# First loads cut smaller and reordered; the output projection's last four weight units kept in two kinds of tiles

## The chip, the cores and the metric

One core of a Trainium2 chip runs the whole kernel. TensorE (PE) multiplies, VectorE (DVE) and ScalarE (ACT) do the elementwise work, GpSimd (POOL) and SyncE (SP) do little more than issue DMAs. The metric is the device time of one execution in microseconds (us). Three runs of the kernel before gave 444.34, 444.35 and 445.06 us; their median is 444.35 us.

## The reference

A two-layer decoder trunk over 256 tokens of width 1024, in float32. Only its two ends matter here:

```python
h = rms_norm(x, norm_g)                  # layer 0 begins
nq, nkc, ..., nz, ... = split(h @ w_in)  # "nz": 512 columns, the gate of the first head group
...
# layer 1 ends: retention output (4 heads x 512) and memory attention (256), gated
y = concat([r_out * silu(rz), m_out * silu(ez)]) @ w_out     # (256, 2304) @ (2304, 1024)
x = x + y
return rms_norm(x, final_norm_g)
```

## The kernel before

Every projection is computed with operands split into a high and a low part: a float32 weight piece arrives in a `raw` tile (six buffers, `NRAW`), ScalarE copies it into a high tile (`S.copy(hi, raw)`, line 122), VectorE subtracts to get the low tile (line 123), and TensorE adds three products, high by high, high by low, low by high (`mm3`, lines 135 to 137). The high and low tiles normally come from the tags `whi` and `wlo`, four buffers each; `split` can be told to take both from another tag, `v4`, which has nine buffers and also serves the residual rows, the last norm's gain and the layer's values and gates.

A scheduler places the instructions in each engine's queue when the kernel is built, from its own estimate of their times; each engine then works through its queue in that order. A tile whose buffers are all taken makes its first writer wait until the oldest one is read for the last time. Only the first loads are placed by hand, inside `tc.manual_schedule` (lines 264 to 279), on the queues of SP and ACT. At most eight loads of these two queues are under way at once: each holds one of eight semaphores, and the ninth waits until the first has landed. The load of `gain0` went through the queue of POOL, which is outside those eight.

**The beginning.** The first projection, "nz" (lines 281 to 293), multiplies 512 columns of weight by the 256 tokens, in eight steps `kt` of 128 rows. For each step `gain_split` (line 233) turns the raw input `xraw` into `xh` (line 237 on VectorE for step 0, line 239 on ScalarE after that) and `xl` (line 240 on VectorE), which needs the gain vector `gain0` (line 245). Before that TensorE runs six warm-up multiplications of a zero tile (line 282), each of which is two instructions in the trace. The second projection, "ksw", is the first that a helper loads: its first two weight pieces are the tiles `ahead` (line 277), and its sums go to the PSUM banks `s`. The loads that follow the weights of "nz" are, in order: vectors, constants, positions, the two pieces `ahead`, and two tiles `xrow` of token rows, whose squares (line 303) give the norm.

**The end.** `out_project` (line 683) multiplies layer 1's 18 units of 128 rows by 1024 output columns. The sums stand in four PSUM banks, `acc[tok][half]`, for two blocks of 128 tokens and two halves of 512 columns; the fourth has the tag `tr`. In the last projection (`last=True`) the last four units are not multiplied when they arrive but kept (`late`, lines 691 to 695), and lines 700 to 705 then go group by group through all four: token block 0, first half; block 0, second half; block 1, first half; block 1, columns 512 to 767; block 1, columns 768 to 1023, which has a bank of its own, `s`. As soon as a group is summed, lines 827 to 861 can take it: add it to the residual (line 839, or 836 for the last group), square it (line 841), multiply by the gain (847), then per token block a root (848), a reciprocal (849), the scaling (851 on GpSimd for block 0, 853 on ScalarE for block 1, 857 and 859 on VectorE) and the stores (860, 861).

The weight tiles of all four kept units have the tag `v4`, two for each unit, eight in all. Two more `v4` tiles hold the residual `x0` and one the gain `gf` at that time.

Of the kernel before, what the change touches and what calls it, by code (L numbers as in the profile page):

```python
# [16 lines left out]
P = 128  # L17
T = 256
D = 1024
KT = 8  # L20
# [23 lines left out]
V_G0 = 0  # L44
# [8 lines left out]
def trunk(  # L53
# [19 lines left out]
    nc = tc.nc  # L73
# [13 lines left out]
    def load(t, src):  # L87
        nc.sync.dma_start(t, src)
        return t
# [28 lines left out]
    def split(raw, cols, tag=None):  # L118

        hi = tl(tag or "whi", [P, 1024], NV if tag else 4, F32R)[:, :cols]  # L120
        lo = tl(tag or "wlo", [P, 1024], NV if tag else 4, F32R)[:, :cols]
        S.copy(hi, raw)  # L122
        V.tensor_tensor(lo, raw, hi.bitcast(F32), ALU.subtract)  # L123
        return hi, lo
# [108 lines left out]
    def gain_split(raw, g, hi, lo, k0, kts):  # L233
        for kt in kts:
            r = raw[:, kt - k0]
            if g is gain0 and kt == 0:
                V.tensor_scalar(hi[:, kt], r, g[:, kt : kt + 1], None, op0=ALU.mult)
            else:
                S.activation(hi[:, kt], r, AF.Copy, scale=g[:, kt : kt + 1])
            V.scalar_tensor_tensor(lo[:, kt], r, g[:, kt : kt + 1], hi[:, kt].bitcast(F32),  # L240
                                   op0=ALU.mult, op1=ALU.subtract)


    gain0 = tl("gain0", [P, KT])
    G.dma_start(gain0, vec[:, V_G0 : V_G0 + KT])
    warm = tl("p", [P, 2, 512], 2)[:, 0]
    V.memset(warm, 0.0)
    seed = tl("seed", [P, 1])
# [13 lines left out]
            xraw.append(tl("raw", [P, 1024], NRAW).rearrange("p (k t) -> p k t", k=4))  # L262
        wraw.append(tl("raw", [P, 1024], NRAW))
    with tc.manual_schedule(engines={mybir.EngineType.SP, mybir.EngineType.Activation}):
        load(wraw[0][:, 0:512], w512[0][:, 0:512])
        nc.scalar.dma_start(xraw[0][:, 0:1], xT[:, 0:1])
        nc.scalar.dma_start(xraw[0][:, 1:2], xT[:, 1:2])
        load(wraw[0][:, 512:1024], w512[0][:, 512:1024])
        S.activation(seed, seed, AF.Sin)
        for q in range(1, 4):  # L270
            load(xraw[q // 2][:, 2 * (q % 2) : 2 * (q % 2) + 2], xT[:, 2 * q : 2 * q + 2])
            load(wraw[q], w512[q // 2][:, (q % 2) * 1024 : (q % 2 + 1) * 1024])
        load(vect, vec)
        load(cpak, cst)
        load(posi, pos)
        load(posr, posrow.to_broadcast([P, T]))
        ahead = [load(tl("raw", [P, 1024], NRAW), w512[2][:, u * 1024 : (u + 1) * 1024]) for u in range(2)]
        for tok in range(2):
            load(xrow[tok], xtok[:, tok])
    wb = bank("t")  # L280
    for _ in range(6):
        PE.matmul(wb[:, :256], warm[:, 0:P], warm[:, :256], start=True, stop=True)
    for q in range(4):
        for j in range(2):
            kt = 2 * q + j
            gain_split(xraw[q // 2], gain0, xh, xl, 4 * (q // 2), (kt,))
            wh, wl = split(wraw[q][:, j * 512 : (j + 1) * 512], 512)
            if kt > 1:
                turned_unit(ps_n, (xh, xl), wh, wl, (kt,), range(4))
                continue  # L290
            for w, x in ((wh, xh), (wh, xl), (wl, xh)):
                for ct in range(4):
                    PE.matmul(ps_n[ct // 2][:, (ct % 2) * T : (ct % 2 + 1) * T], w[:, ct * P : (ct + 1) * P], x[:, kt],
                              start=kt == 0 and ct % 2 == 0 and w is wh and x is xh, stop=False, skip_group_check=True)

    rstd0 = tl("rstd0", [P, 2])
    rq0 = tl("rq0", [P, 2])
# [381 lines left out]
    def out_project(first, ys, last=False):  # L679

        acc = [[bank("pj"), bank("pj")], [bank("pj"), bank("tr")]]
        todo = []
        for y, n in ys:
            for k0 in range(0, n, 2):
                todo.append((y, k0))
        total = len(todo)
        kept = []
        for i, (y, k0) in enumerate(todo):
            for u in range(2):
                raw = load(tl("raw", [P, 1024], NRAW), wout[first + i][:, u * 1024 : (u + 1) * 1024])  # L690
                late = last and i >= total - 2
                wh, wl = split(raw, 1024, "v4" if late else None)
                if late:
                    kept.append((y, k0 + u, wh, wl))
                    continue
                for tok in range(2):
                    for c in range(2):
                        part(acc, tok, c * 512, 512, y, k0 + u, wh, wl, i == 0 and u == 0,
                             not last and i == total - 1 and u == 1)
        if last:  # L700
            rest = bank("s")
            for tok, c0, n in ((0, 0, 512), (0, 512, 512), (1, 0, 512), (1, 512, 512 - CUT), (1, 1024 - CUT, CUT)):
                for j, k in enumerate(kept):
                    dst = [[rest, rest]] * 2 if c0 + CUT == D else acc
                    part(dst, tok, c0, n, *k, c0 + CUT == D and j == 0, j == len(kept) - 1)
            acc.append(rest)
        return acc
# [256 lines left out]
```

## Time and profile before

| | us |
|---|---|
| median of three runs | 444.35 |
| profiled execution, whole | 444.3 |
| profiled execution, span from first to last instruction | 442.5 |
| TensorE busy | 427.5 (97%) |
| VectorE busy | 312.5 (71%) |
| ScalarE busy | 250.3 (57%) |

The span is 1.8 us shorter than the time of the same execution; what lies around it is launch and end. "Busy" is the time in which an instruction ran; matmuls overlap, so a busy TensorE is not one at its peak. The chain that ended last lies to 90% on TensorE, which means that nearly all of the span is one engine's queue. In timelines, "[idle before <-releaser]" says how long the engine had been idle ahead of the row and what ended it. The tile names leave the buffer numbers out, and some lose their digits: `v` is the tag `v4`, `gain` is `gain0`.

### The profile page before, as it was taken

To read this page: it belongs to the slowest core of one execution; us is meant where nothing else is said; L and a number is where in the kernel's file an instruction comes from. 1 tells how busy PE (TensorE), PEld (TensorE's weight loads), DVE (VectorE), ACT (ScalarE), POOL (GpSimd) and SP (SyncE) were. 2 spreads that over 40 slices of the span, in tenths; PEclk is the share of its full clock that TensorE was granted. 3 is DMA by queue.
4 is the path that set the end of the run, shared out by engine and by line. 5 is a ranking of instruction groups with operands and counts; after the bars stand their busy time and mean duration, and the time that the engine had idled before them with its cause. 6 is when DMAs were issued, how large, how long until landed. Compare 5 with 4: busy or idle time off the path is not lost.

```text
span 442.5 us, 6757 instructions
## 1 busy us (share of the span) xinstructions
PE 427.5 (97%) x2450; PEld 353.8 (80%) x2450; DVE 312.5 (71%) x734; ACT 250.3 (57%) x463; POOL 4.2 (1%) x10
## 2 busy tenths in 40 slices
PE   8999999999999899999999999999999999999991
PEld 7988999788776577669987878888888888888871
DVE  4899695995578765739688874676998467586315
ACT  5775537765649866837566544556355535546123
POOL 1000000000000000000000000000000000000001
PEclk9999999999999999999999999999999999999997
DMA  8975956654435314334464454655466553656002
GB/s 270 391 265 171 381 164 204 221 184 128 157 97 198 135 47 144 96 107 130 146 209 138 148 177 142 189 175 191 129 207 200 171 168 121 230 191 190 1 0 95
DMA packets 30081, 74.22 MB, mean 168 GB/s; under 512 B 2784, under 2 KB 14048, under 8 KB 30048
## 3 DMA queue, kind: packets, MB, share of 16 engines
q1 hardware_dynamic: 29584, 73.27, 50.3%
q10 hardware_dynamic: 432, 0.52, 0.4%
q8 instruction: 19, 0.31, 0.3%
q14 instruction: 14, 0.11, 0.1%
q0 software_dynamic: 32, 0.00, 0.0%
HBM read 72.74 MB, written 1.05 MB: 167 GB/s over the span
## 4 chain that ended last, share of the span: by engine, by line
PE 90%; DVE 4%; DMA 2%; ACT 1%; issue 1%; POOLq 0%; ACTq 0%
PE pj L136 18%; PE pj L135 17%; PE pj L137 17%; PE pj L181 8%; PE pj L182 4%; PE t L216 4%; PE s L100 4%; PE o L100 3%; PE tr L136 1%; PE tr L135 1%; DVE wlo L123 1%; DMA raw<-in_memtok 1%; PE tr L137 1%; PE s L136 1%; PE s L135 1%; PE s L137 1%
## 5 line engine op out<-in xcount | busy, mean ns | idle before, releaser
L123 DVE TENSOR_TENSOR wlo<-raw,whi 128x1024 fp32r<-128x1024 f32 (+2 forms) x124 | 144.6, 1172 | 59.8 <-ACT whi L122 58.5
L122 ACT CAST whi<-raw 128x1024 fp32r<-128x1024 f32 (+2 forms) x124 | 124.7, 1009 | 91.8 <-PE pj L137 40.4
L136 PE MATMUL pj<-wlo,big 128*128 128x512 f32 (+2 forms) x264 | 99.5, 377 | 0.1
L137 PE MATMUL pj<-whi,big 128*128 128x512 f32 (+2 forms) x264 | 98.2, 373 | 0.0
L135 PE MATMUL pj<-whi,big 128*128 128x512 f32 (+2 forms) x264 | 98.2, 375 | 0.0
L137 PEld LDWEIGHTS pj<-whi,big 128*128 128x128 f32 x264 | 49.7, 188 | 8.7 <-issue 0.3
L135 PEld LDWEIGHTS pj<-whi,big 128*128 128x128 f32 x264 | 49.7, 188 | 8.7 <-DVE wlo L123 0.4
L181 PE MATMUL pj<-big,whi 128*128 128x512 f32 x160 | 56.6, 397 | 0.0
L136 PEld LDWEIGHTS pj<-wlo,big 128*128 128x128 f32 x264 | 49.7, 188 | 8.6 <-DVE wlo L123 0.3
L182 PE MATMUL pj<-big,wlo 128*128 128x256 f32 x160 | 44.7, 283 | 0.0
L181 PEld LDWEIGHTS pj<-big,whi 128*128 128x128 f32 x160 | 29.8, 188 | 6.7 <-DVE tmp L356 0.3
L135 PE MATMUL pj<-big,whi 128*128 128x256 f32 x120 | 34.4, 288 | 0.1
L136 PE MATMUL pj<-big,whi 128*128 128x256 f32 x120 | 34.4, 287 | 0.0
L137 PE MATMUL pj<-big,wlo 128*128 128x256 f32 x120 | 34.1, 284 | 0.0
L182 PEld LDWEIGHTS pj<-big,wlo 128*128 128x128 f32 x160 | 30.2, 189 | 1.1 <-issue 0.7
L135 PEld LDWEIGHTS pj<-big,whi 128*128 128x128 f32 x120 | 22.8, 191 | 0.9 <-DVE v L723 0.5
L136 PEld LDWEIGHTS pj<-big,whi 128*128 128x128 f32 x120 | 22.9, 191 | 0.8 <-issue 0.7
L137 PEld LDWEIGHTS pj<-big,wlo 128*128 128x128 f32 x120 | 22.9, 191 | 0.0
L405 ACT ACTIVATE p<-p,mx 128x128 f32<-128x128 f32 (+1 forms) x48 | 21.3, 447 | 0.9 <-DVE mx L403 0.9
L417 ACT COPY pt<-t 128x384 f32<-128x384 f32 x24 | 11.5, 479 | 18.1 <-PE t L216 18.0
L216 PE MATMUL t<-cst,p 128*128 128x128 f32 x104 | 18.1, 284 | 0.6 <-ACT pt L417 0.6
L123 DVE TENSOR_TENSOR v<-raw,v 128x1024 fp32r<-128x1024 f32 x4 | 4.9, 1225 | 19.1 <-ACT v L122 19.1
(297 smaller groups left out, 656.8 us busy)
## 6 DMA issues: line engine op xcount, KB each, us to landing
raw<-in_w SPq DMA_DIRECT2D x91, 512.0 KB, 4.2
raw<-in_wout SPq DMA_DIRECT2D x28, 512.0 KB, 3.9
v<-in_xtok SPq DMA_DIRECT2D x4, 512.0 KB, 7.2
raw<-in_w SPq DMA_DIRECT2D x4, 280.0 KB, 3.6
v<-in_w SPq DMA_DIRECT2D x2, 512.0 KB, 6.9
raw<-in_memT SPq DMA_DIRECT2D x2, 512.0 KB, 4.8
raw<-in_memtok SPq DMA_DIRECT2D x2, 512.0 KB, 4.8
v<-in_grow SPq DMA_DIRECT2D x2, 512.0 KB, 7.3
```

The source lines that it names most:

```text
L100: ins = PE.matmul(out, lhs, rhs, start=start, stop=stop)
L122: S.copy(hi, raw)
L123: V.tensor_tensor(lo, raw, hi.bitcast(F32), ALU.subtract)
L135: PE.matmul(ps, lh, rh, start=start, stop=False, skip_group_check=shared)
L136: PE.matmul(ps, lh, rl, start=False, stop=False, skip_group_check=shared)
L137: PE.matmul(ps, ll, rh, start=False, stop=stop, skip_group_check=shared)
L181: PE.matmul(ps[ct], wh[:, c], both[:, :, kt], start=kt == 0, stop=False, skip_group_check=True)
L182: PE.matmul(ps[ct][:, T:], wl[:, c], both[:, 0, kt], start=False, stop=kt == KT - 1, skip_group_check=True)
L216: PE.transpose(b[:, i * P : (i + 1) * P], a, ident)
L405: S.activation(p[:, hh, a], p[:, hh, a], AF.Exp, bias=mx[:, hh, tok : tok + 1], scale=-1.0, accum_out=sm[:, hh, tok : tok + 1])
L417: got = S.copy(pt[:, hh, :384], transposes([p[:, hh, i * P : (i + 1) * P] for i in range(3)]))
```

## The change

Five edits at the beginning and one at the end.

- `gain0` is loaded first on ACT's queue instead of on POOL's.
- The weights of step 0 (256 KB) come in two pieces of 256 columns, the first on ACT's queue, the second on SP's. The inputs of steps 0 and 1 come on SP's queue instead of ACT's, and the input of step 0 is the first load there.
- The warm-up is three multiplications instead of six.
- Step 0 is split and multiplied in two halves of 256 columns (`first_columns`); step 1 goes through the same function whole.
- `gain_split` and `split` stand in one loop over `kt`, with the same calls for steps 2 to 7.
- In the last output projection only the units of the last pair of rows (`i == total - 1`) take `v4` tiles. The first two kept units take `whi` and `wlo`.

```diff
--- before.py
+++ after.py
@@ -242,7 +242,6 @@
 
 
     gain0 = tl("gain0", [P, KT])
-    G.dma_start(gain0, vec[:, V_G0 : V_G0 + KT])
     warm = tl("p", [P, 2, 512], 2)[:, 0]
     V.memset(warm, 0.0)
     seed = tl("seed", [P, 1])
@@ -262,9 +261,11 @@
             xraw.append(tl("raw", [P, 1024], NRAW).rearrange("p (k t) -> p k t", k=4))
         wraw.append(tl("raw", [P, 1024], NRAW))
     with tc.manual_schedule(engines={mybir.EngineType.SP, mybir.EngineType.Activation}):
-        load(wraw[0][:, 0:512], w512[0][:, 0:512])
-        nc.scalar.dma_start(xraw[0][:, 0:1], xT[:, 0:1])
-        nc.scalar.dma_start(xraw[0][:, 1:2], xT[:, 1:2])
+        nc.scalar.dma_start(gain0, vec[:, V_G0 : V_G0 + KT])
+        load(xraw[0][:, 0:1], xT[:, 0:1])
+        nc.scalar.dma_start(wraw[0][:, 0:256], w512[0][:, 0:256])
+        load(wraw[0][:, 256:512], w512[0][:, 256:512])
+        load(xraw[0][:, 1:2], xT[:, 1:2])
         load(wraw[0][:, 512:1024], w512[0][:, 512:1024])
         S.activation(seed, seed, AF.Sin)
         for q in range(1, 4):
@@ -278,20 +279,26 @@
         for tok in range(2):
             load(xrow[tok], xtok[:, tok])
     wb = bank("t")
-    for _ in range(6):
+    for _ in range(3):
         PE.matmul(wb[:, :256], warm[:, 0:P], warm[:, :256], start=True, stop=True)
-    for q in range(4):
-        for j in range(2):
-            kt = 2 * q + j
-            gain_split(xraw[q // 2], gain0, xh, xl, 4 * (q // 2), (kt,))
-            wh, wl = split(wraw[q][:, j * 512 : (j + 1) * 512], 512)
-            if kt > 1:
-                turned_unit(ps_n, (xh, xl), wh, wl, (kt,), range(4))
-                continue
-            for w, x in ((wh, xh), (wh, xl), (wl, xh)):
-                for ct in range(4):
-                    PE.matmul(ps_n[ct // 2][:, (ct % 2) * T : (ct % 2 + 1) * T], w[:, ct * P : (ct + 1) * P], x[:, kt],
-                              start=kt == 0 and ct % 2 == 0 and w is wh and x is xh, stop=False, skip_group_check=True)
+    def first_columns(w, kt, c0, n):
+
+        wh, wl = split(w, n)
+        for a, x in ((wh, xh), (wh, xl), (wl, xh)):
+            for ct in range(c0 // P, (c0 + n) // P):
+                PE.matmul(ps_n[ct // 2][:, (ct % 2) * T : (ct % 2 + 1) * T], a[:, ct * P - c0 : ct * P - c0 + P], x[:, kt],
+                          start=kt == 0 and ct % 2 == 0 and a is wh and x is xh, stop=False, skip_group_check=True)
+
+    for kt in range(KT):
+        w = wraw[kt // 2][:, (kt % 2) * 512 : (kt % 2 + 1) * 512]
+        gain_split(xraw[kt // 4], gain0, xh, xl, 4 * (kt // 4), (kt,))
+        if kt == 0:
+            for c0 in (0, 256):
+                first_columns(w[:, c0 : c0 + 256], 0, c0, 256)
+        elif kt == 1:
+            first_columns(w, 1, 0, 512)
+        else:
+            turned_unit(ps_n, (xh, xl), *split(w, 512), (kt,), range(4))
 
     rstd0 = tl("rstd0", [P, 2])
     rq0 = tl("rq0", [P, 2])
@@ -689,7 +696,7 @@
             for u in range(2):
                 raw = load(tl("raw", [P, 1024], NRAW), wout[first + i][:, u * 1024 : (u + 1) * 1024])
                 late = last and i >= total - 2
-                wh, wl = split(raw, 1024, "v4" if late else None)
+                wh, wl = split(raw, 1024, "v4" if last and i == total - 1 else None)
                 if late:
                     kept.append((y, k0 + u, wh, wl))
                     continue
```

How this moves the instructions, from the order in which each engine gets them. The line numbers of the changed kernel are seven higher behind line 300.

SP's queue at the start, before; raw_77 holds the weights of steps 0 and 1, raw_76 the inputs of steps 0 to 3, raw_78 and raw_79 the next ones of each:

```order
L88 DMA raw_77<-in_w 128x512 x2
L88 DMA raw_76<-in_xT 128x512
L88 DMA raw_78<-in_w 128x1024
L88 DMA raw_79<-in_xT 128x512
L88 DMA raw_80<-in_w 128x1024
L88 DMA raw_79<-in_xT 128x512
```

and in the changed kernel, where raw_76 holds the first weights and raw_75 the first inputs:

```order
L88 DMA raw_75<-in_xT 128x256
L88 DMA raw_76<-in_w 128x256
L88 DMA raw_75<-in_xT 128x256
L88 DMA raw_76<-in_w 128x512
L88 DMA raw_75<-in_xT 128x512
L88 DMA raw_77<-in_w 128x1024
L88 DMA raw_78<-in_xT 128x512
L88 DMA raw_79<-in_w 128x1024
```

The input of step 0 comes first; the input of steps 2 and 3 (raw_75, 128x512) is the fifth issue instead of the third, and all that follows moves back by two in the same way. ACT's queue at the same place, before:

```order
L266 DMA raw_76<-in_xT 128x256
L267 DMA raw_76<-in_xT 128x256
L269 ACT_TABLE_LOAD
L269 ACTIVATE seed_65<-seed_65 128x1
L122 CAST whi_115<-raw_77 128x512
```

and now:

```order
L264 DMA gain_1_61<-in_vec 128x8
L266 DMA raw_76<-in_w 128x256
L270 ACT_TABLE_LOAD
L270 ACTIVATE seed_64<-seed_64 128x1
L122 CAST whi_113<-raw_76 128x256
L122 CAST whi_123<-raw_76 128x256
L239 ACTIVATE big_72<-raw_75,gain_1_61 128x256
L122 CAST whi_135<-raw_76 128x512
```

The gain and a quarter of the first weights take the place of two inputs, and the first cast is now two of 256 columns.

TensorE's last rows, before; v_847, v_850 and v_853 are the high tiles of the second, third and fourth kept unit, v_848, v_851 and v_854 their low tiles, pj_4024 and pj_4025 token block 0, s_4304 the last group:

```order
L135 MATMUL s_4304<-v_850_4294,y_3938 128x256
L136 MATMUL s_4304<-v_851_4295,y_3938 128x256
L137 MATMUL s_4304<-v_850_4294,y_3938 128x256
L135 MATMUL pj_4024<-v_853_4300,y_3938 128x512
L135 MATMUL pj_4025<-v_853_4300,y_3938 128x512
L135 MATMUL pj_4026<-v_853_4300,y_3938 128x512
L135 MATMUL tr_4027<-v_853_4300,y_3938 128x256
L135 MATMUL s_4304<-v_853_4300,y_3938 128x256
L136 MATMUL pj_4024<-v_854_4301,y_3938 128x512
L137 MATMUL pj_4024<-v_853_4300,y_3938 128x512
L136 MATMUL pj_4025<-v_854_4301,y_3938 128x512
L137 MATMUL pj_4025<-v_853_4300,y_3938 128x512
```

All groups go through three units; the fourth unit's fifteen matmuls stand behind the last group, its five high-by-high ones first. In the changed kernel, where pj_4026 is block 0's first half, the kept units are whi_4284, whi_4290, v_852 and v_855:

```order
L135 MATMUL pj_4026<-whi_4284,y_3940 128x512
L136 MATMUL pj_4026<-wlo_4285,y_3940 128x512
L137 MATMUL pj_4026<-whi_4284,y_3940 128x512
L135 MATMUL pj_4026<-whi_4290,y_3940 128x512
L135 MATMUL pj_4027<-whi_4284,y_3940 128x512
L136 MATMUL pj_4027<-wlo_4285,y_3940 128x512
L136 MATMUL pj_4026<-wlo_4291,y_3940 128x512
L137 MATMUL pj_4026<-whi_4290,y_3940 128x512
L135 MATMUL pj_4026<-v_852_4296,y_3940 128x512
L136 MATMUL pj_4026<-v_853_4297,y_3940 128x512
L137 MATMUL pj_4026<-v_852_4296,y_3940 128x512
L135 MATMUL pj_4026<-v_855_4302,y_3940 128x512
```

The four units now stand inside one group, and the group pj_4026 is finished before the next ones begin (two matmuls of pj_4027 stand in front). ScalarE's last casts, before:

```order
L122 CAST v_847_4288<-raw_4286 128x1024
L122 CAST whi_4228<-raw_4226 128x1024
L122 CAST v_850_4294<-raw_4292 128x1024
L795 CAST y_3938<-t_4015 128x4x128
L122 CAST whi_4246<-raw_4244 128x1024
L122 CAST whi_4264<-raw_4262 128x1024
L122 CAST v_853_4300<-raw_4298 128x1024
L825 ACT_TABLE_LOAD
L825 ACTIVATE root_4365<-root_4365 128x1
```

and now:

```order
L122 CAST v_852_4296<-raw_4294 128x1024
L802 CAST y_3940<-t_4017 128x4x128
L122 CAST whi_4248<-raw_4246 128x1024
L122 CAST v_855_4302<-raw_4300 128x1024
L832 ACT_TABLE_LOAD
L832 ACTIVATE root_4367<-root_4367 128x1
L122 CAST whi_4266<-raw_4264 128x1024
L122 CAST whi_4284<-raw_4282 128x1024
L122 CAST whi_4290<-raw_4288 128x1024
```

Before, the last cast is that of the fourth kept unit into v_853; now the two `v4` casts come early, and the last three casts fill `whi` tiles, two of them kept units. VectorE's rows behind its last split, before:

```order
L839 TENSOR_TENSOR v_388_2025<-pj_4024,v_388_2025 128x512
L839 TENSOR_TENSOR v_388_2025<-pj_4025,v_388_2025 128x512
L847 TENSOR_TENSOR p_4369<-v_388_2025,v_796_4022 128x512
L839 TENSOR_TENSOR v_389_2027<-pj_4026,v_389_2027 128x512
L839 TENSOR_TENSOR v_389_2027<-tr_4027,v_389_2027 128x512
L843 TENSOR_SCALAR ss_857_4368<-ss_857_4368 128x1
L847 TENSOR_TENSOR p_4385<-v_389_2027,v_796_4022 128x512
L847 TENSOR_TENSOR p_4385<-v_389_2027,v_796_4022 128x256
L843 TENSOR_SCALAR ss_861_4384<-ss_861_4384 128x1
L836 TENSOR_TENSOR v_389_2027<-s_4304,v_389_2027 128x256
L849 RECIPROCAL ss_857_4368<-ss_857_4368 128x1
```

and now:

```order
L846 TENSOR_TENSOR v_390_2027<-pj_4026,v_390_2027 128x512
L854 TENSOR_TENSOR p_4371<-v_390_2027,v_798_4024 128x512
L850 TENSOR_SCALAR ss_859_4370<-ss_859_4370 128x1
L846 TENSOR_TENSOR v_390_2027<-pj_4027,v_390_2027 128x512
L856 RECIPROCAL ss_859_4370<-ss_859_4370 128x1
L864 SCALAR_TENSOR_TENSOR p_4371<-v_390_2027,ss_859_4370,v_798_4024 128x512
L846 TENSOR_TENSOR v_391_2029<-pj_4028,v_391_2029 128x512
L854 TENSOR_TENSOR p_4387<-v_391_2029,v_798_4024 128x512
L846 TENSOR_TENSOR v_391_2029<-tr_4029,v_391_2029 128x512
L850 TENSOR_SCALAR ss_863_4386<-ss_863_4386 128x1
L854 TENSOR_TENSOR p_4387<-v_391_2029,v_798_4024 128x256
L843 TENSOR_TENSOR v_391_2029<-s_4306,v_391_2029 128x256
```

Before, both halves of block 0 are added one right behind the other and their reciprocal (849) comes after the last group's add (836). Now each group's add is followed by its own work, and the reciprocal of block 0 (now 856) stands ahead of block 1.

## Rows read from the trace of the kernel before

**Rows 1.** page, part 1: busy us (share of span) and instructions by engine.

```profile
PE 427.5 (97%) x2450; PEld 353.8 (80%) x2450; DVE 312.5 (71%) x734; ACT 250.3 (57%) x463; POOL 4.2 (1%) x10
```

**Rows 2.** timeline, TensorE, 0 to 25 us: start, us, engine, line, operation, tiles, count.

```profile
1.46 5.49 PE L282 MATMUL t<-p 128*128 128x256 f32 x12 [1.46 <-DVE root L824]
6.54 1.72 PE L293 MATMUL pj<-big,whi 128*128 128x256 f32 x8
8.10 0.64 PE L293 MATMUL pj<-big,wlo 128*128 128x256 f32 x4
...
18.54 0.28 PE L137 MATMUL pj<-big,wlo 128*128 128x256 f32 x1
...
19.13 0.39 PE L136 MATMUL s<-wlo,big 128*128 128x512 f32 x1
...
24.59 0.39 PE L136 MATMUL s<-wlo,big 128*128 128x512 f32 x1
```

**Rows 3.** timeline, VectorE and then ScalarE, 4 to 24 us.

```profile
6.04 0.35 DVE L237 TENSOR_SCALAR big<-raw,gain 128x256 fp32r<-128x256 f32 x1 [4.62 <-DMA gain<-in_vec]
...
17.34 1.22 DVE L123 TENSOR_TENSOR wlo<-raw,whi 128x1024 fp32r<-128x1024 f32 x1
...
23.00 1.23 DVE L123 TENSOR_TENSOR wlo<-raw,whi 128x1024 fp32r<-128x1024 f32 x1
...
8.31 1.15 ACT L122 CAST whi<-raw 128x512 fp32r<-128x512 f32 x2 [0.71 <-DMA raw<-in_w]
...
16.19 1.05 ACT L122 CAST whi<-raw 128x1024 fp32r<-128x1024 f32 x1 [2.30 <-DMA raw<-in_w]
...
20.16 1.06 ACT L303 ACTIVATE v<-v 128x1024 f32<-128x1024 f32 x1 [0.37 <-DMA v<-in_xtok]
```

**Rows 4.** busy time by stretch: PE, PEld, DVE, ACT, POOL, PEclk, DMA share, GB/s.

```profile
8.00:20.00 12.00, 12.00 (x97) 11.78 (x96) 11.02 (x24) 8.34 (x14) 0.00 (x0) 1.00 1.03 388
...
432.95:442.50 9.55, 0.00 (x0) 0.00 (x0) 4.90 (x14) 3.51 (x12) 2.04 (x1) 0.75 0.29 110
```

**Rows 5.** timeline, TensorE, 420 to 433 us.

```profile
420.66 0.39 PE L135 MATMUL pj<-v,y 128*128 128x512 f32 x1
...
426.94 0.28 PE L135 MATMUL tr<-v,y 128*128 128x256 f32 x1
...
428.96 0.28 PE L137 MATMUL s<-v,y 128*128 128x256 f32 x1
...
429.55 0.96 PE L135 MATMUL pj<-v,y 128*128 128x512 f32 x3 [0.31 <-ACT v L122]
...
432.66 0.28 PE L137 MATMUL s<-v,y 128*128 128x256 f32 x1
```

**Rows 6.** timeline, ScalarE, 408 to 430 us.

```profile
408.90 2.00 ACT L122 CAST whi<-raw 128x1024 fp32r<-128x1024 f32 x2
...
428.44 1.05 ACT L122 CAST v<-raw 128x1024 fp32r<-128x1024 f32 x1 [17.54 <-PE s L136]
```

**Rows 7.** timeline, VectorE and SyncE, 431 to 439 us.

```profile
435.63 0.41 DVE L836 TENSOR_TENSOR v<-s,v 128x256 f32<-128x256 f32 x1
...
436.93 1.43 SPq L861 DMA_DIRECT2D out_y<-p  x2
438.45 0.38 SPq L860 DMA_DIRECT2D out_y<-p  x1
```

**Rows 8.** the tile out_y, its four DMAs.

```profile
DMA to landing us min/median/max: 2.0/2.7/2.9
```

**Rows 9.** DMA issues, 0 to 20 us: line, engine, count, KB, us to landing.

```profile
raw<-in_xT ACTq DMA_DIRECT2D x1, 128.0 KB, 3.6
...
gain<-in_vec POOLq DMA_DIRECT2D x1, 4.0 KB, 4.8
```

**Rows 10.** DMA queues, 0 to 20 us: packets, MB, share of 16 engines.

```profile
q1 hardware_dynamic: 2609, 6.20, 87.5%
q10 hardware_dynamic: 288, 0.26, 4.5%
```

## The prediction, made before the changed kernel was run

> **What bounds the kernel now.** The page's first part comes first: TensorE is busy for 97% of the span [rows 1], so only the stretches count in which its queue stands, and whatever lies behind its last matmul. The timeline of its two ends shows both places of the change. At the beginning, the warm-up covers 5.49 us from 1.46, and the first real matmul starts at 6.54 [rows 2]. VectorE's timeline says what that one waits for: its first product idles 4.62 us until the gain has landed, and runs from 6.04 to 6.39 [rows 3]. From 6.54 on TensorE does not pause, but it is followed closely: the low part of the first "ksw" piece is ready at 17.34 + 1.22 = 18.56 and used at 19.13, that of the third piece is ready at 23.00 + 1.23 = 24.23 and used at 24.59 [rows 2, 3]. Those are spare times of 0.57 and 0.36 us. What paces these two is not TensorE: the first cast waited 2.30 us for its load until 16.19, the squares of the token rows waited for theirs until 20.16 [rows 3], and the 16 DMA engines are full from 8 to 20 us at 388 GB/s [rows 4].
>
> At the end, the kept units' matmuls run from 420.66; 27 of 512 columns take until 426.94 (0.2326 each), 17 of 256 until 428.96 (0.1188 each). Then TensorE waits: the three that begin at 429.55 are those of the fourth unit, and the last of its fifteen starts at 432.66 [rows 5]. ScalarE says why: it had been idle 17.54 us, until the group `s` had read an older tile, when it began the fourth unit's cast at 428.44 [rows 6]. Nothing in the tail could start earlier, since every group needs that unit. So VectorE's adds come one behind the other after TensorE's end, the last at 435.63, and SP's last store at 438.45 [rows 7]. Behind the last matmul 9.55 us of span are left without TensorE, with 4.90 us of VectorE's work in them [rows 4].
>
> **The end of the change.** Four kept units need eight `v4` tiles where six were free. Now two of them take four, and two take `whi` and `wlo`. No instruction is added. Sixty matmuls run without a pause: 36 x 0.2326 + 23 x 0.1188 = 11.11, so the last starts at 431.77, 0.89 us earlier than 432.66, and ends 0.28 later at 432.05 [rows 5].
>
> The larger part lies behind it. Block 0's groups are summed 24 and more matmuls before the end, that is by 420.66 + 24 x 0.2326 + 0.2 = 426.4; its adds, root, scaling and stores then run beside block 1's 5.6 us of matmuls. All of the tail's VectorE work is 4.90 us [rows 4], of which block 0 has about half, so it fits there. I cost it at nothing; uncovered it would cost up to 2.5. Only the last group's add is left to wait for TensorE, and can begin at 432.05 instead of 435.63: 3.58 us earlier [rows 5, 7]. What follows it is unchanged up to block 1's stores. The second one of SP's two issues starts at about 436.93 + 1.43 - 0.36 = 438.0, now 434.4. SP's store at 438.45, which waited for GpSimd's 2.04 us [rows 4, 7], belongs to block 0 and is early now. A store lands 2.0 to 2.9 us after its issue, 2.7 in the middle [rows 8]. Before, the end was 438.45 + 2.9 = 441.35, with 1.15 of span behind it; now 434.4 + 2.7 + 1.15 = 438.25. The end gives 442.5 - 438.25 = 4.25, bounded by 3.6 (only the add's shift) and 4.9 (a landing after 2.0). I take 4.2.
>
> The added waits are those of the two `whi` casts, which wait for the unit four places ahead of them. Each unit is twelve matmuls, 2.79 us, so the second one's wait ends at 420.66 - 2 x 2.79 = 415.1. A cast of 1.05 and a split of 1.22 [rows 3, 6] make 417.4, 3 us ahead of need. Between 410.9 and 428.44 ScalarE had nothing to do [rows 6]; that hides all the casts. Behind them in its queue there are only the squares of the tail. The table load moved ahead of three casts runs in the same idle stretch.
>
> **The beginning.** The warm-up's half ends at 1.46 + 5.49 / 2 = 4.2. The gain leaves POOL's queue, where it took 4.8 us from issue to landing, for ACT's, where the 128 KB issued first took 3.6 [rows 9]; issued at the start it is there by about 4.3 at the latest. So the first real matmul can start between 4.2 and 4.8, about 2 us earlier. But steps 2 and 3 need a load whose cast began at 8.31 and whose first half ends 0.6 later [rows 3]. With the same bytes ahead of it, step 2 starts at about 8.9, where now it starts at 8.10 + 16 x 0.120 = 10.02 (0.120 is 10.44 us over the 87 matmuls up to 18.54) [rows 2]. That lead of 1.1 us shrinks to 0.57 at the first "ksw" piece and to 0.36 at the third, since neither load has fewer bytes ahead of it. With a few hundredths for the hand-over I take 0.3. Behind that TensorE decides alone, and the lead is kept to the end.
>
> For the smaller pieces: the first 20 us moved 6.20 MB in q1, rows of 2 KB and more for the most part, for 87.5% of 320 us, 45 us per MB; q10's rows of 1 KB cost 4.5% of 320 us for 0.26 MB, 55 us per MB [rows 10]. The 256 KB that now come in 1 KB rows cost 0.26 x 10 / 16 = 0.17 us of the stream at most, nothing at least. I take nothing, since q1's figure contains the stalls of the start as well. The Trainium skill (DMA: Bandwidth & Descriptors, Rules for kernel authors) speaks against this half of the change: small transfers should be merged, and issuing from another engine saves only issue time, as all queues share 16 engines. By that rule alone the beginning would give nothing and the time would be 440.1; the full engines [rows 4] agree with it for everything behind step 2.
>
> The gain now holds one of the eight load semaphores, so SP waits one load sooner: the inputs of steps 4 and 5 wait for the gain, and all later loads stand behind them. The eight loads ahead hold 1.5 MB, 4 us of work at 388 GB/s [rows 4], so the engines do not run dry.
>
> **Sum.** The profiled execution has 444.3 us, 1.8 around its span; the median is 444.35. 444.3 - 4.2 - 0.3 = 439.8.
>
> **Rivals.**
> 1. *The full clock comes later.* From 6.54 to 8.10 a matmul takes 0.195, later 0.120 [rows 2], with a granted clock of 1.00 behind 8 us, the level of 2.4 GHz [rows 4]; so part of the first stretch ran at the lower level, 1.2 GHz, at 0.24 at most. The warm-up is halved, and a pause may follow it. If the full level needs the present 6.6 us (1.46 to 8.10) from 4.4 on, it comes at 11. From 4.4 on at 0.24, TensorE falls behind the old schedule after 9.9, half a us for each one: 0.5 us lost instead of 0.3 gained, 440.6. Against it: the gap is short. The Trainium skill (TensorE: Matmul & The Clock Gate, Part 1) says that the lower clock is the default and sustained activity releases it; the fall from 0.195 to 0.120 agrees, and no pause ahead of it is to be seen in this trace.
> 2. *The loads come earlier.* The first 20 us moved 6.46 MB, of which 12 x 0.388 = 4.66 fall behind 8 us [rows 4, 10], so the first 8 us moved only 1.8 MB; if the gain's small transfer on POOL's queue or the order held it back, "ksw" moves up too, and the lead of 1.1 us is kept: 439.0. Nothing but the slow start speaks for it.
> 3. *The end is held back.* ScalarE's queue has the last `v4` cast, which waits for the last load, ahead of the three `whi` casts. If that load is late, the casts are too, and TensorE pauses inside the groups; or the fourth unit still comes last and the change does not do what it says. Half of the 4.2 is lost: 442; all of it: 444. Against it stands 3 us of spare time.
> 4. *Slower.* The lower clock stays through "ksw", because the loads leave pauses in TensorE's first work. Each us behind 9.9 costs 0.5; the change is slower from 9.9 + 4.2 / 0.5 = 18.3 us on, and at 20 the time is 445.2. After 8.10 the kernel before shows no such stretch.
>
> **Chances.** Forecast 0.52 (439.4 to 440.2), first rival 0.20, second 0.15, third 0.09, slower 0.04. A third of the third rival ends within 0.2% (0.9 us, about what can be told from no change). That gives faster 0.93, same 0.03, slower 0.04. The range runs from 438.8 to 441.3: it takes in both ends of the store's landing and the first rival.
>
> **What would show it.** In the changed profile TensorE has no wait between the first kept matmul and its end, and the last matmul starts some 11.1 us after the first; behind it about 6.2 us of span are left instead of 9.55. The first real matmul starts before 5 us. The second "ksw" low-part matmul row (19.13 here) is 0.3 to 0.6 earlier, and the same lead is still there at the first kept matmul. I am wrong if that lead is gone in the middle, if TensorE pauses in the kept groups, or if block 0's stores are issued after block 1's matmuls end.

## The result, and the profile after

The changed kernel takes 440.48 us (median of five runs, 440.16 to 441.16) against 444.48 for the kernel before beside it (444.34 to 445.06): a ratio of 0.9911, 95% interval 0.990 to 0.9923. Forecast were 439.8, and 438.8 to 441.3. The profiled execution took 440.28, its span 438.5. TensorE's work is the old one less six warm-up instructions, page part 1:

```profile
PE 426.3 (97%) x2444; PEld 352.7 (80%) x2444; DVE 314.3 (72%) x735; ACT 250.7 (57%) x464; POOL 3.5 (1%) x9
```

**The end did what was forecast.** The timelines of TensorE, ScalarE, VectorE and SyncE there answer to [rows 5 to 7]:

```profile
420.99 0.40 PE L135 MATMUL pj<-whi,y 128*128 128x512 f32 x1
...
432.09 0.28 PE L137 MATMUL s<-v,y 128*128 128x256 f32 x1
...
415.57 1.05 ACT L122 CAST whi<-raw 128x1024 fp32r<-128x1024 f32 x1 [0.99 <-PE tr L137]
425.20 0.64 ACT L848 ACTIVATE rot_a<-v 128x512 f32<-128x512 f32 x1 [8.58 <-DVE v L846]
...
432.41 0.42 DVE L843 TENSOR_TENSOR v<-s,v 128x256 f32<-128x256 f32 x1 [0.25 <-PE s L137]
...
429.59 0.35 SPq L868 DMA_DIRECT2D out_y<-p  x1
...
434.77 0.33 SPq L868 DMA_DIRECT2D out_y<-p  x1
```

Sixty matmuls start within 11.10 us (420.99 to 432.09) with no wait among them. ScalarE makes its last kept cast at 415.57 and then idles 8.58 us; the cast at 428.44 of [rows 6] is gone. Block 0's first store is issued at 429.59, while TensorE works on block 1. Only the last group's add stands behind TensorE (432.41, formerly 435.63). Behind the last matmul 6.12 us are left instead of 9.55, with 1.40 us of VectorE's work instead of 4.90 [rows 4]:

```profile
432.37:438.49 6.12, 0.00 (x0) 0.00 (x0) 1.40 (x5) 1.52 (x4) 0.00 (x0) 0.74 0.26 98
```

**The beginning lost.** The first kept matmul comes at 420.99, 0.33 later than the 420.66 of [rows 5], where 0.3 earlier was forecast. TensorE's, VectorE's and ScalarE's timelines of the first 20 us, beside [rows 2, 3] (VectorE's row stands behind TensorE's):

```profile
1.45 2.93 PE L283 MATMUL t<-p 128*128 128x256 f32 x6 [1.45 <-DVE root L831]
5.04 2.07 PE L289 MATMUL pj<-big,whi 128*128 128x256 f32 x8 [0.66 <-ACT whi L122]
...
9.09 0.64 PE L289 MATMUL pj<-big,wlo 128*128 128x256 f32 x4
10.27 0.39 PE L135 MATMUL pj<-big,whi 128*128 128x256 f32 x1 [0.54 <-ACT whi L122]
...
19.72 0.40 PE L136 MATMUL s<-wlo,big 128*128 128x512 f32 x1
...
3.31 0.35 DVE L237 TENSOR_SCALAR big<-raw,gain 128x256 fp32r<-128x256 f32 x1 [1.90 <-DMA gain<-in_vec]
...
9.60 1.14 ACT L122 CAST whi<-raw 128x512 fp32r<-128x512 f32 x2 [0.43 <-DMA raw<-in_w]
...
17.20 1.05 ACT L122 CAST whi<-raw 128x1024 fp32r<-128x1024 f32 x1 [2.44 <-DMA raw<-in_w]
```

The gain is there by 3.3 us and the first real matmul, which now waits for the cast of the first weights, starts at 5.04, 1.5 earlier. But the weights of steps 2 and 3 are first cast at 9.60 instead of 8.31, step 2 starts at 10.27 instead of 10.02, and the "ksw" row, the first matmul there that reads a low weight part and a landmark for all that follows, comes at 19.72 instead of 19.13. The chain of waits names the load (start, us, what):

```profile
0.73 0.38 SPq L88
1.17 0.42 SPq L88
1.64 0.42 SPq L88
2.11 0.43 SPq L88
2.58 0.43 SPq L88
3.06 6.52 DMA raw<-in_w
9.60 0.63 ACT whi L122
10.27 0.39 PE pj L135
```

Five issues of SyncE, 0.47 us apart, stand ahead of it, so the load goes out at 3.06. In the kernel before three did, and it went out at 2.12 (SyncE's timeline there):

```profile
1.66 0.42 SPq L88 DMA_DIRECT2D raw<-in_xT  x1
2.12 0.43 SPq L88 DMA_DIRECT2D raw<-in_w  x1
```

And between 5 and 7.5 us the engines moved 308 GB/s before (first line) and 194 now (second; the last three columns are TensorE's granted clock, DMA share, GB/s):

```profile
5.00:7.50 2.50, 2.50 (x9) 2.00 (x8) 1.46 (x4) 1.93 (x4) 0.00 (x0) 1.00 1.04 308
```

```profile
5.00:7.50 2.50, 2.46 (x11) 2.46 (x12) 1.62 (x4) 1.33 (x3) 0.00 (x0) 1.00 0.86 194
```

### The profile page after: what moved, and what is told of

The parts are those of the page before. It is cut to its first block, busy times and chain, and to the rows that moved or that the text cites. A ratio compares the mean times of both kernels' runs of the same rounds, so it can differ in the third digit from the quotient of the medians.

```text
span 438.5 us, 6749 instructions
## 1 busy us (share of the span) xinstructions
PE 426.3 (97%) x2444; PEld 352.7 (80%) x2444; DVE 314.3 (72%) x735; ACT 250.7 (57%) x464; POOL 3.5 (1%) x9
## 4 chain that ended last, share of the span: by engine, by line
PE 95%; DMA 1%; ACT 1%; SPq 0%; DVE 0%; issue 0%; DVEq 0%
PE pj L135 19%; PE pj L136 19%; PE pj L137 19%; PE pj L181 9%; PE s L100 5%; PE pj L182 4%; PE t L216 4%; PE o L100 3%; DMA raw<-in_w 1%; PE tr L136 1%; PE tr L135 1%; PE s L136 1%; PE s L137 1%; PE s L135 1%; PE tr L137 1%; PE s L775 1%
## 5 line engine op out<-in xcount | busy, mean ns | idle before, releaser
L123 DVE TENSOR_TENSOR wlo<-raw,whi 128x1024 fp32r<-128x1024 f32 (+3 forms) x127 | 147.3, 1165 | 65.5 <-ACT whi L122 64.3
L122 ACT CAST whi<-raw 128x1024 fp32r<-128x1024 f32 (+3 forms) x127 | 126.8, 1003 | 94.4 <-PE pj L137 40.9
L182 PE MATMUL pj<-big,wlo 128*128 128x256 f32 x160 | 44.7, 283 | 0.0
L137 PE MATMUL pj<-big,wlo 128*128 128x256 f32 x120 | 33.2, 285 | 0.0
L410 DVE CUSTOM_DVE_ANT_0 p<-s,cst 128x128 f32<-128x128 f32 (+1 forms) x48 | 14.3, 353 | 5.6 <-PE t L216 5.1
```

The lines of the kernel that those rows point to most:

```text
L137: PE.matmul(ps, ll, rh, start=False, stop=stop, skip_group_check=shared)
L182: PE.matmul(ps[ct][:, T:], wl[:, c], both[:, 0, kt], start=False, stop=kt == KT - 1, skip_group_check=True)
L410: V.tensor_tensor_reduce(p[:, hh, a], ss[hh][tok], cpak[:, C_CAUSAL + a.start : C_CAUSAL + a.stop], -1.0, 3e38, ALU.add, ALU.min, mx[:, hh ...
```

## The experiments

Eleven kernels ran, each timed in five rounds beside the kernel before, whose medians in the three sessions were 444.24, 444.26 and 444.43. One table serves them all. "Issue" and "cast" are those of the load for steps 2 and 3, "ksw" is the row described above, "rest" is the span behind it; all but the median are read from the profiled execution.

| kernel | issue | cast | step 2 | ksw | rest | median us |
|---|---|---|---|---|---|---|
| before | 2.12 | 8.31 | 10.02 | 19.13 | 423.4 | 444.48 |
| changed | 3.06 | 9.60 | 10.27 | 19.72 | 418.8 | 440.48 |
| end alone | 2.13 | 8.24 | 9.87 | 18.98 | 419.0 | 440.07 |
| beginning alone | 3.06 | 9.76 | 10.43 | 19.88 | 422.9 | 444.81 |
| one unit moved | 2.13 | 8.59 | 9.61 | 18.95 | 418.9 | 440.11 |
| warm-up of six | 3.06 | 9.89 | 10.56 | 20.01 | 419.1 | 440.68 |
| SyncE's count as before | 2.12 | late (10.1) | 13.57 | 22.68 | 418.7 | 442.97 |
| step 0's weights whole | 2.58 | 8.79 | 10.58 | 19.69 | 418.8 | 440.39 |
| two tiny loads | 3.07 | 9.15 | 9.82 | 19.45 | 419.0 | 441.47 |
| gain first | 2.12 | late (9.3) | 10.83 | 20.14 | 419.0 | 439.92 |
| inputs in one | 2.11 | 8.83 | 9.64 | 19.19 | 418.9 | 440.10 |
| gain third | 2.12 | late (8.8) | 14.36 | 23.83 | 419.0 | 443.69 |
| all merged | 2.11 | 8.52 | 11.45 | 20.61 | 419.0 | 442.17 |

"Late" means that ScalarE came to this cast late because an earlier instruction in its queue waited; in brackets stands when the load itself had landed, its issue plus its time to landing in the DMA issues of the trace (8.0, 7.2 and 6.7 us). The rest is 418.7 to 419.1 with the new end and 422.9 to 423.4 with the old one, whatever the beginning: the two halves of the change add up, and a beginning is worth what its ksw row says. (The rows of a line can stand apart from its median: the profiled execution of the two tiny loads was their fastest, 440.17, that of the gain first its slowest, 440.91, that of the gain third took 444.64 and that of all merged 441.38.)

**The end alone.** The kernel before with one edit:

```diff
-                wh, wl = split(raw, 1024, "v4" if late else None)
+                wh, wl = split(raw, 1024, "v4" if last and i == total - 1 else None)
```

> The kernel before with the change's end alone (two kept units in whi and wlo); the loads at the start as before. Theory A (the end gave 4.3 us, the start took 0.3 back): 440.1 us, 0.4 below the whole change; first kept matmul near 420.7 as before, and the third ksw piece's first low-part matmul near 24.6. Rival B (the start gave the forecast 0.3 and the end only 3.7): 440.8, above the whole change.

440.07 (439.81 to 440.29), ratio 0.9902, interval 0.989 to 0.9915: 4.17 us faster than 444.24. The end gives all of the gain: the whole change gave 4.00 beside its own kernel before, and the two intervals overlap.

**The beginning alone.** The changed kernel with `"v4" if late` again.

> The changed kernel's start alone; the four kept units all in v4 tiles as before. Theory A: 444.8, no gain or some 0.3 us slower than before; the first ksw matmul near 19.2 instead of 18.66. Rival B: 444.2, some 0.3 us faster, with the first ksw matmul before 18.66.

444.81 against 444.24, ratio 1.001, interval 1.0001 to 1.0019: the beginning costs 0.57 by this pair, an interval that only just leaves out zero. The changed kernel against the end alone gives 0.41 from the medians, or 0.17 when each is taken against the kernel before of its own session. It does not gain; the size of the loss is not known better than that. Here the chain of waits does not lead to the late load but through steps 0 and 1:

```profile
1.18 3.34 DMA raw<-in_w
4.55 0.41 ACT whi L122
5.01 5.40 PE pj L289 x24
10.43 0.39 PE pj L135
```

Twenty-four matmuls take 5.40 us, 0.225 each, where 0.120 is the later pace [rows 2]. So two limits lie close together: the load, and a TensorE that works slowly so early. The granted clock does not show why it is slow: it reads 1.00 from 5 to 7.5 us in the changed kernel (row above) while the matmuls go at half the later pace.

**One unit moved.** The kernel before with three units in `v4` and one in `whi` and `wlo`:

```diff
+                wh, wl = split(raw, 1024, "v4" if late and i + u > total - 2 else None)
```

> The kernel before with one kept unit (the first) in whi and wlo instead of two; three stay in v4 tiles, which need six, as many as are free. Theory A (the whole loss at the end was one unit waiting for two tiles): the full gain of the end, 440.1, with no wait of ScalarE for the group s. Rival C (the gain needs both units moved, since v4 tiles come free late or in the wrong order): a wait stays in the kept groups and the time lies between 441 and 444.

440.11 (439.64 to 440.91), not to be told from 440.07 with two units moved. Six `v4` tiles were free, and the unit that found none was the whole stall. No cast on ScalarE waits for TensorE any more (its timeline; the next instruction there is the tail's at 423.89):

```profile
410.35 1.28 ACT L825 ACT_TABLE_LOAD   x1
411.64 0.20 ACT L825 ACTIVATE root<-root 128x1 f32<-128x1 f32 x1
411.75 1.98 ACT L122 CAST whi<-raw 128x1024 fp32r<-128x1024 f32 x2
```

**The warm-up of six.** The changed kernel with `for _ in range(6)`.

> The changed kernel with six warm-up multiplications again. Theory A (the later load stream is what the start lost): no difference that can be told, 440.3 to 440.6, first ksw matmul again 0.5 or more behind 18.66. Rival D (the halved warm-up left TensorE at the lower clock for longer and that cost the start): 0.4 to 0.6 us faster than the whole change, 440.0, and the first ksw matmul at or before 18.7.

440.68 (440.24 to 440.87). TensorE now does steps 0 and 1 at nearly the later pace, and then waits for the load:

```profile
5.90 1.30 PE L289 MATMUL pj<-big,whi 128*128 128x256 f32 x8
...
10.56 0.38 PE L135 MATMUL pj<-big,whi 128*128 128x256 f32 x1 [1.45 <-ACT whi L122]
```

The longer warm-up mends the pace. The slow pace alone is not what lost the lead: with it mended the time does not fall, as theory A expects and rival D (440.0) does not.

**SyncE's count as before.** The changed kernel, its four small loads dealt out otherwise:

```diff
-        load(xraw[0][:, 0:1], xT[:, 0:1])
-        nc.scalar.dma_start(wraw[0][:, 0:256], w512[0][:, 0:256])
-        load(wraw[0][:, 256:512], w512[0][:, 256:512])
-        load(xraw[0][:, 1:2], xT[:, 1:2])
+        nc.scalar.dma_start(xraw[0][:, 0:1], xT[:, 0:1])
+        load(wraw[0][:, 0:256], w512[0][:, 0:256])
+        nc.scalar.dma_start(wraw[0][:, 256:512], w512[0][:, 256:512])
+        nc.scalar.dma_start(xraw[0][:, 1:2], xT[:, 1:2])
```

> The changed kernel with the four small first loads dealt out otherwise: ScalarE's queue issues the gain, both single input tiles and the second half of step 0's weights, SyncE's queue only the first half, so that SyncE again issues two loads ahead of those for steps 2 and 3, as in the kernel before. Pieces, their number and the halved warm-up stay. Theory A (SyncE issues one load in 0.47 us, and the two added ones make every later load 0.93 us late): the second weight load is issued at 2.1 instead of 3.06, its first cast starts at 8.3 to 8.7 instead of 9.60, TensorE has no wait ahead of step 2, the second low-part row of the first weights behind step 7 (19.72 in the changed kernel) comes at 18.7 to 19.1, and the time is 439.7 to 440.0. Theory B (eight loads may be outstanding, and small ones fill the eight with fewer bytes) and theory C (rows of 1 KB move more slowly): nothing moves, first cast 9.3 to 9.7, 440.4 to 440.6.

442.97: all three theories missed. The load for steps 2 and 3 went out at 2.12, as theory A asks, but it took 8.0 us and landed at 10.1, later than in the changed kernel (DMA issues from 2.07 to 2.52 us):

```profile
raw<-in_w SPq DMA_DIRECT2D x1, 512.0 KB, 8.0
```

The third load on ScalarE's queue, 128 KB issued at 1.66, landed 7 us later, and ScalarE and TensorE stood (chain of waits, then the DMA queues from 4.5 to 8.5 us, q1 SyncE's and q10 ScalarE's):

```profile
1.66 7.03 DMA raw<-in_w
8.72 0.41 ACT whi L122
```

```profile
q1 hardware_dynamic: 345, 0.90, 77.3%
q10 hardware_dynamic: 258, 0.23, 16.8%
```

The two queues get packets in similar number, 345 and 258, but SyncE's hold 2.6 KB in the mean and ScalarE's 0.9, so SyncE's queue moves four times the bytes. The Trainium skill (DMA: Bandwidth & Descriptors, Queues, rings and completion order) says that each engine takes turns between its queues packet by packet; these counts roughly agree.

**Step 0's weights whole.** The changed kernel with one load of 256 KB on ScalarE's queue in place of the two pieces, one issue of SyncE less:

```diff
-        nc.scalar.dma_start(wraw[0][:, 0:256], w512[0][:, 0:256])
-        load(wraw[0][:, 256:512], w512[0][:, 256:512])
+        nc.scalar.dma_start(wraw[0][:, 0:512], w512[0][:, 0:512])
```

> The changed kernel with step 0's weights as one load of 256 KB in rows of 2 KB on ScalarE's queue, so SyncE has one issue less and the rows are those of the kernel before. Theory A (SyncE's issues): half of the delay is gone, the second weight load is issued at 2.6, its first cast starts at 8.8 to 9.2, 440.1 to 440.3. Theory B (bytes in the eight outstanding loads, 1.80 MB instead of 1.54): about a third gone, first cast 9.2, 440.3. Theory C (rows of 1 KB): all of it gone, first cast 8.3 to 8.6, 439.8 to 440.0.

Issue at 2.58, cast at 8.79: the row is theory A's (8.8 to 9.2), and theories B (9.2) and C (8.3 to 8.6) miss it. The time, 440.39, is above all three, since the load was no longer the limit: the first real matmul starts at 5.87, and 24 slow ones end at 10.74.

```profile
8.79 0.62 ACT L122 CAST whi<-raw 128x512 fp32r<-128x512 f32 x1 [0.78 <-DMA raw<-in_w]
```

**Two tiny loads.** The end alone, and `for spare in spares: load(spare, vec[:, V_G0 : V_G0 + KT])` ahead of the loads for steps 2 and 3, two tiles of 4 KB.

> The kernel before with the end changed, and two needless loads of 4 KB that SyncE issues ahead of the loads for steps 2 and 3: no piece is smaller, nothing is in another order, 8 KB more are moved. To be compared with 440.07 of the end alone. Theory A (SyncE's issues): the second weight load is issued at 3.06, its first cast starts at 9.0 to 9.4 instead of 8.24, the time is 440.2 to 440.6. Theory B (the two take two of the eight places): the engines move 50 to 110 KB in half a microsecond between 6 and 7.5 us, as in the changed kernel, where they move 140 to 190 otherwise; first cast 9.3 to 9.6, 440.4 to 440.6. Theory C (rows of 1 KB): nothing, first cast 8.2 to 8.5, 440.0 to 440.2.

```profile
9.15 0.62 ACT L122 CAST whi<-raw 128x512 fp32r<-128x512 f32 x1 [0.33 <-DMA raw<-in_w]
```

Two issues with next to no bytes, no smaller piece, no other order, and the cast starts at 9.15 instead of 8.24, 0.91 later, while the way from issue to landing stays at 6.1 us: theory A's row. Theory C, which expected nothing, cannot explain it. Theory B's mark is not where it was expected (297 GB/s from 5 to 7.5), but a thin stretch comes behind it, 230 GB/s from 7.5 to 10 against 392 with the end alone. The time, 441.47 (440.17 to 442.07), is above all of them; only the fastest execution is in the trace, so what the others lost isn't shown.

**The gain first.** The end alone, and the gain as ScalarE's first issue instead of GpSimd's.

> The kernel before with the end changed, and of the beginning only one thing: the gain is the first issue of ScalarE's queue instead of GpSimd's. Pieces, SyncE's list and the warm-up are those of the kernel before. All three theories: the load stream is that of the kernel before (first cast of the second weight load 8.2 to 8.6), since SyncE's list is. The first real matmul starts at 5.9 to 6.0, right behind the warm-up, steps 0 and 1 end at about 9.0, step 2 starts at 9.0 to 9.4, the second low-part row behind step 7 comes at 18.5 to 18.9, and the time is 439.5 to 439.9, below both the change (440.48) and the end alone (440.07). If the lead is lost at that row or behind it, as it stands 0.57 and 0.36 us ahead of its loads in the kernel before, it is 440.0 to 440.2.

439.92 (439.64 to 440.91), ratio 0.9903, interval 0.9886 to 0.992: not to be told from the end alone. In the profiled execution, the slowest of the four, step 2 starts at 10.83 and not at the expected 9.0 to 9.4: the inputs of step 1, now ScalarE's third issue, are the limit:

```profile
1.66 6.94 DMA raw<-in_xT
8.69 0.52 ACT big L239
9.25 1.74 PE pj L293 x12
```

**The inputs in one load.** The end alone; ScalarE issues the inputs of steps 0 and 1 as one load and then the gain.

> The kernel before with the end changed; ScalarE's queue issues the inputs of steps 0 and 1 as one load of 256 KB (two of 128 KB in the kernel before) and then the gain (from GpSimd's queue there). SyncE's list, the number of loads ahead of each later one, and the warm-up are those of the kernel before. Theory A (every issue ahead of a load on SyncE's queue costs it 0.47 us, and nothing else in the beginning matters for it): first cast of the second weight load at 8.1 to 8.5; gain and inputs landed by 5.4, so the first real matmul starts behind the warm-up at 5.9 to 6.3 without a later wait, steps 0 and 1 end at 8.9 to 9.4, the first ksw matmul starts at 17.7 to 18.2, and the time, 419.5 and 1.8 behind that matmul, is 439.0 to 439.6. Rival D (what ScalarE's queue moves beside SyncE's lands late, as the third load there did in the run with the gain first): the single input load lands at 6 to 8, the lead is lost, first ksw matmul 18.4 to 19.5, 440.0 to 440.8.

440.10. Theory A's 439.0 to 439.6 failed, and so did its cast (8.83 against 8.1 to 8.5): the gain landed at 6.1 and the first real matmul started at 6.71, 0.84 behind the warm-up. Rival D's time held; its mark did not quite, since the inputs landed at 5.1 and only the gain behind them came after 6.

**The gain third.** The end alone; ScalarE issues the two inputs and then the gain.

> The kernel before with the end changed, and the gain as the third issue of ScalarE's queue, behind the two input loads, instead of GpSimd's. It is one more of the eight loads that may be outstanding, so SyncE's load for steps 4 and 5 waits for the first load and is issued at 4.1 instead of 3.07. Theory A: second weight load as in the kernel before (cast 8.2 to 8.5), gain landed at 4.5 to 5.5 instead of 5.7 to 5.97, first real matmul at 5.9 to 6.3, steps 0 and 1 end at 9.2 to 9.6 as the second input load sets them, first ksw matmul 18.0 to 18.4, 439.3 to 439.9. Theory B (a later issue by the limit of eight leaves the engines with too little): they move under 110 KB in some half microseconds between 5 and 8, first ksw matmul 18.8 to 19.5, 440.2 to 440.8. Rival D (loads on ScalarE's queue land late): the gain lands at 7 to 8.6, no better than 440.5.

443.69 (441.26 to 445.59). The gain landed at 7.96, rival D's mark, TensorE idled 2.55 us behind the warm-up, and then its granted clock was down (chain of waits, TensorE's timeline, and windows of TensorE and the others; PEclk is the third number from the end):

```profile
1.66 6.30 DMA gain<-in_vec
```

```profile
8.57 1.20 PE L293 MATMUL pj<-big,whi 128*128 128x256 f32 x4 [2.55 <-ACT big L239]
```

```profile
7.50:10.00 2.50, 1.27 (x5) 1.00 (x5) 1.76 (x5) 1.95 (x5) 0.00 (x0) 0.67 1.04 404
10.00:15.00 5.00, 5.00 (x23) 5.00 (x24) 3.99 (x9) 3.23 (x7) 0.00 (x0) 0.50 1.05 392
15.00:17.50 2.50, 2.50 (x22) 2.50 (x22) 0.97 (x2) 0.62 (x1) 0.00 (x0) 0.96 1.02 411
```

At 0.50, the level of 1.2 GHz, TensorE started 23 matmuls in 5 us, 0.217 each. That is nearly the pace of steps 0 and 1 with the changed beginning, where the column reads 1.00. The twelve executions of this kernel lie far apart and go with the clock: 441.26 us at a mean granted clock of 0.997, 445.59 at 0.987.

**All merged.** The changed kernel with the inputs of steps 0 and 1 as one load on SyncE's queue and step 0's weights as one on ScalarE's.

> The changed kernel with its small pieces merged again: SyncE issues the inputs of steps 0 and 1 as one load of 256 KB, ScalarE's queue the gain and then step 0's weights as one of 256 KB. SyncE has two issues less than in the changed kernel and one less than in the run with step 0's weights whole. Theory A: the second weight load is issued at 2.1 and its first cast starts at 8.2 to 8.6 (9.60 with 3.06, 8.79 with 2.58). The warm-up is the short one and step 0's weights land at about 5.4 as in that run, so the first real matmul starts at 5.8 to 6.0 and most of steps 0 and 1 runs at the lower clock: they end at about 10.5, first ksw matmul 18.9 to 19.2, 440.2 to 440.5. Theory C (rows of 1 KB move slowly; none is left): first cast before 8.0. Theory that the load stream is late for another reason than its issues (GpSimd's queue is empty, or the stall of the engines at 5 to 7 us): first cast 9.0 or later.

Issue at 2.11, load landed at 8.5, cast at 8.52: theory A's row again. But step 0's weights landed at 6.5, TensorE had paused 2.64 us, and its 24 matmuls took 4.63 us from 7.02: 442.17, above every expectation.

**What follows.** Over the runs in which the cast waited for its load, it starts at 8.24 to 8.83 when the load is issued at 2.1, at 8.79 with 2.58, and at 9.15 to 9.89 with 3.1. In the changed kernel SyncE waits for no landing in its first 7 us, so the 0.94 us by which its load goes out later are those of the two added issues. That is theory A, and the two tiny loads show the same price with next to no bytes; they take two of the eight places as well, but SyncE's first wait for one comes behind the load in question. But the issue is not all. The way from issue to landing is 6.1 to 6.8 us in these runs, and 6.7, 7.2 and 8.0 in the three marked late, where ScalarE's queue issues three or four loads and not two: with SyncE's count restored the load landed later still. That ScalarE's further loads make that way longer fits these three, but in each of them something else changed as well, so it is not shown.

The rest, up to 0.7, goes with the thin stretch behind 5 us, seen in all three kernels with the changed loads untouched (194, 181 and 166 GB/s), not with step 0's weights whole (296), and 2.5 us later with the two tiny loads, whose weights come in the old rows. So the rows alone don't make it. Whether the bytes in the eight outstanding loads do stays open: SyncE's count as before has as few of them (1.54 MB) and moved 278, and all merged, with 2.3 MB, had a thin stretch from 2.5 to 5 us (176 GB/s). No beginning tried here is measurably better than that of the kernel before. The end alone, one line, at 440.07, is as good as any version measured.

## Why the prediction was right, and where it was wrong

- **The end, 4.2 forecast: right.** It measures 4.17, and each row came out: 11.1 us from first to last matmul, 6.1 us left behind and block 0 stored beside block 1's matmuls. That block 0's sums cost nothing is shown by VectorE's 4.90 us that became 1.40.
- **The beginning, 0.3 gained: wrong**, it loses 0.2 to 0.6. The step that failed is "steps 2 and 3 need a load whose cast began at 8.31 ... With the same bytes ahead of it, step 2 starts at about 8.9". The bytes were the same, the issues were not. SyncE issued its first loads 0.47 us apart whatever their size (4 to 512 KB in these runs), and the edit moved two more onto its queue; the row for that is the one of SyncE's timeline shown above. That is 0.94 of the 1.29 us by which the cast came later; the rest is a longer way from issue to cast, 6.54 us instead of 6.19, and goes with the thin stretch.
- The same step took for granted that TensorE would be done with steps 0 and 1 by 8.9. Starting at 5.0 with a short warm-up it needs 4.7 to 5.4 us for them and ends at 9.7 to 10.4. So the load on time alone would hardly have paid either (in the beginning alone the chain of waits leads through these matmuls to 10.43), nor did the faster pace alone (warm-up of six): each of the two takes the lead away.
- **"The engines do not run dry"** was wrong: 194 GB/s and a busy share of 0.86 from 5 to 7.5 us. What the smaller pieces cost, put at nothing, no run tests alone.
- **First rival, the full clock comes later, 440.6:** its price was near, 440.48. The slow pace behind the shorter warm-up was there, but mending it gained nothing, and that the clock was the reason is not shown: the granted clock reads 1.00 from 5 to 7.5 us in both kernels (rows above). **Second, the loads come earlier:** the reverse. **Third, the end is held back,** and **fourth, slower:** no.
- The Trainium skill (DMA: Bandwidth & Descriptors, Rules for kernel authors), weighed as a rule against this half, would have given 440.1. The end alone, which is that result, took 440.07, but the changed beginning was not neutral, and merging its pieces again, as the rule advises, took 442.17 (all merged). The rule that issuing from another engine only saves issue time does not tell all of the first 8 us here: the second half of step 0's weights, 128 KB, landed 3.2 us after its issue on SyncE's queue in the changed kernel and 7.0 after it as the third load on ScalarE's.

The forecast missed by 440.48 - 439.8 = 0.7: the 0.3 that did not come, and some 0.4 lost instead. The end carries the result; the beginning's sign was wrong, and the prediction's own mark for that came true, since the lead was gone at the ksw row (19.72 against 19.13) and the first real matmul started at 5.04 and not before 5.

## What to carry to other kernels

When a stall comes from a ring of tiles that is too short by a few, count the free ones: moving one unit to another kind of tile gave 4.13 us, all of the end's gain within the noise. When loads are cut or moved between queues, write down each later load's place in its issuing queue and multiply by the issue time, before any count of bytes; then look at what the other queue moves beside it, since a restored place did not bring the load back here. And an earlier start of the first consumer is worth only what the second one's data and TensorE's pace then allow.

## What the runs showed of the hardware that was not expected

- At the start, a place later in ScalarE's queue costs far more than an issue. The gain (4 KB) landed between 3.3 and 5.4 us as its first load (changed kernel, all merged), at 6.1 behind a load of 256 KB, and at 7.96 as the third, behind two of 128 KB; on GpSimd's queue it landed at 5.6 to 6.0. All had been issued by 1.7 us.
- A pause of 2.55 us behind the warm-up was followed by a granted clock of 0.50 from 10 to 15 us, which with the wait itself put the ksw row 4.85 us behind that of the end alone.
